# Chunk-causal encoder block: the queries of the next pair of heads are projected, split and stacked before the attention of the current pair

## Chip, cores and metric

One core of one Trainium2 chip runs the whole kernel in one launch. The metric is the device time of that launch in microseconds (us). Three runs of the kernel before have a median of 711.69 us (704.27 to 712.39).

## The reference, cut to what matters

One layer of an encoder on 512 tokens of width 1024. A modulated norm gives `u`; `u @ w_in` gives the inputs of a retention branch and of a sparse-attention branch ("DSA"); both go through output projections and gates into `w_o`; then comes a mixture of 16 experts and a last norm. The change touches the sparse attention alone. For a block of 128 queries it computes:

```python
kg = jax.vmap(lambda a, i: a[i])(k, sel)      # the selected keys
logits = jnp.einsum('bqhd,bqkd->bqhk', qb, kg).astype(jnp.float32) * (dh ** -0.5)
logits = logits + jnp.transpose(bias, (0, 1, 3, 2))
logits = jnp.where(valid[:, :, None, :], logits, -jnp.inf)
p = jax.nn.softmax(logits, axis=-1).astype(vg.dtype)
return jnp.einsum('bqhk,bqkd->bqhd', p, vg)
```

There are 8 heads of 64 columns, one latent key and value set for all heads, and 512 queries and keys. The queries of the heads are `u @ w_in[:, C_DQ:]`.

## The kernel before, in words

Everything is recorded first and ordered afterwards. Code in `block` calls engine operations through `Engine`; `Program.record` notes each one with its dependences and with a priority, which is its place in the recording plus `R.shift`. `Program.run` then plans: it takes each engine's ready operations by time and priority, with a cost for each instruction and each transfer written in the kernel, gives buffers their places, and issues all instructions from one line (L494). So every instruction has the line L494 in the profile, every SBUF tile is called `arena`, every PSUM tile `banks`, and a group is told by its shape. An engine works through its instructions strictly in the planned order. Nearly all transfers are issued by SyncE (SP), in one planned order as well.

Weights come from memory in float32, 1 MB at a time (`chunk`). `split` turns a chunk into two float16 halves (high and low): per 1024 columns one ScalarE (ACT) copy and one VectorE (DVE) subtraction. A product is then three float16 matmuls (`mm3`), and a projection of 128 columns for all 512 tokens is 24 matmuls of 128x512 (`z_T`).

The stage around the change (lines 961 to 1064) runs over four pairs of heads, and `dsa(pr, wqh, wql)` does one pair:

- `z_T` projects the pair's queries into a PSUM bank (line 964: 24 matmuls), and `hi_lo_psum` (line 966) writes the high half with ACT and the low half with DVE.
- `stack_q` (line 967) moves both halves into the stacked tile `dq` by four SBUF-to-SBUF transfers of 64 KB, so that one matmul with 128 rows multiplies the high and the low half together. In the profile these are `arena<-arena` transfers.
- A 0.5 MB transfer loads the pair's bias (line 969).
- For each of four blocks of 128 queries: four logit matmuls into a single double bank (lines 977, 978; tile `tL`, one buffer), bias added on DVE (980), mask and maximum on DVE (984), two exponentials (987) and two scalings (991) on ACT, transposes on TensorE (996), copies on ACT (997), and products with the values on TensorE (1000). The shapes of a block are 128x128, 128x256, 128x384 and 128x512 wide, since later queries see more keys.

Between these the planner lays other work, recorded after `dsa(pr)` with a later priority: `ret_out(pr)` (two new weight chunks, `w_gate` and `w_ret_out`; per pair 48 matmuls of the gates and 48 of the retention output, with a tanh) and two `mod_row` (each loads 2 MB of `w_ada` and sums it on DVE). After the four pairs come the second half of the gates with `w_dsa_out`, then `w_o`, the router and the experts. There are two buffers each for `dq`, for the halves (`tDH`) and for the PSUM banks of `psa`, which are given out in the order of recording. The loop before:

```python
    for pr in range(4):
        if pr % 2 == 0:
            wq = chunk([w_in[:, :, C_DQ + pr * 128:C_DQ + (pr + 2) * 128]])
        dsa(pr, *wq)
        R.shift, R.patience = 300, 0.0
        ret_out(pr)
        R.shift = 250
        for q in range(2):
            mod_row(pr, q)
        R.shift, R.patience = 0, 25
```

Of the kernel before, what the change touches and what calls it, by code (L numbers as in the profile page):

```python
# [31 lines left out]
C_RQ, C_RK, C_RV, C_RG, C_DQ, C_DKV, C_IQ, C_IK, C_IW, C_END = (  # L32
    0, 512, 1024, 2048, 3072, 3584, 3712, 4224, 4288, 4296)
# [470 lines left out]
def block(ctx, tc, A, out):  # L504
# [13 lines left out]
    def stt(o, a, s, b, op0, op1, **k):  # L518
        return DVE.scalar_tensor_tensor(o, a, s, b, op0=op0, op1=op1, **k)
# [18 lines left out]
    w_in = A["w_in"].rearrange("l (k p) n -> p (l k) n", p=128)  # L538
# [78 lines left out]
    def psa():  # L617
        return T(tA, [512])

    def psf():  # L620
        return T(tF, [512])
# [22 lines left out]
    def raw_tile():  # L644
        return T(tW8, [2048], F32, "raw", 1)

    def split(raw, n=2048, tag=tW8):
        hl = T(tag, [2, 2048], F16, "hl")
        wh, wl = hl[:, 0], hl[:, 1]
        for a in range(0, n, 1024):  # L650
            b = min(n, a + 1024)
            r, h, l = raw[:, a:b], wh[:, a:b], wl[:, a:b]
            ACT.activation(h, r, AF.Copy, scale=WS)
            stt(l, r, WS, h, OP.mult, OP.subtract)
        return wh, wl

    def chunk(parts, tag=tW8):
        raw = raw_tile()
        n = 0
        for src in parts:  # L660
            m = src.shape[1] * src.shape[2]
            SP.dma_start(raw[:, n:n + m].rearrange("p (k n) -> p k n", n=src.shape[2]), src)
            n += m
        return split(raw, n, tag=tag)
# [19 lines left out]
    for c in "aaawwawwwwww":  # L684
        if c == "a":
            ra = T(tADA, [8, 2, 256])
            n = len(ada) * 256
# [44 lines left out]
    for j in range(KT):  # L732
        wh, wl = split(wr[j], 712)
        for m in range(6):
            a, n = m * 128, widths[m]
# [24 lines left out]
    def hi_lo_psum(ps, scale, hi, lo):  # L760
        ACT.activation(hi, ps, AF.Copy, scale=scale)
        stt(lo, ps, scale, hi, OP.mult, OP.subtract)

    def stack_q(dst, hi, lo):
        SP.dma_start(dst[0:64, 0], hi[0:64])
        SP.dma_start(dst[64:128, 0], lo[0:64])
        SP.dma_start(dst[64:128, 1], lo[64:128])
        SP.dma_start(dst[0:64, 1], hi[64:128])
# [7 lines left out]
    def z_T(wh, wl, c0, cn, ps):  # L776
        for k in range(KT):
            mm3(ps, wh[:, k * cn + c0:k * cn + c0 + 128], wl[:, k * cn + c0:k * cn + c0 + 128],
                uh[:, k], ul[:, k], k == 0, k == KT - 1)
# [178 lines left out]

    R.patience = 25

    def dsa(pr, wqh, wql):
        dq = T(tDQ, [2, S], F16)
        p = psa()
        z_T(wqh, wql, (pr % 2) * 128, 256, p)
        hl = T(tDH, [2, S], F16)
        hi_lo_psum(p, IWS, hl[:, 0], hl[:, 1])
        stack_q(dq, hl[:, 0], hl[:, 1])
        bt = T(tBT, [2, S])
        SP.dma_start(bt, bass.AP(tensor=bias_rep.tensor, offset=bias_rep.offset + 2 * pr * 640 + 127,
                                 ap=[[8 * 640 - 1, 128], [640, 2], [1, S]]))  # L970
        po = psa()
        for b in range(NT):
            W = 128 * (b + 1)
            p = T(tL, [2, 512])
            for i in range(2):
                q = dq[:, i, b * 128:(b + 1) * 128]
                PE.matmul(p[:, i, :W], q, dkh[:, :W], start=True, stop=False)
                PE.matmul(p[:, i, :W], q, dkl[:, :W], start=False, stop=True)
            t = T(tLG, [2, S])
            stt(t[:, :, :W], p[:, :, :W], 0.125, bt[:, :, 384 - 128 * b:512], OP.mult, OP.add)  # L980
            sm = T(tSX, [3, 2])

            for i in range(2):
                DVE.tensor_tensor_reduce(t[:, i, :W], t[:, i, :W], am[b], scale=-1.0, scalar=BIG, op0=OP.add, op1=OP.min,
                                         accum_out=sm[:, 0, i:i + 1])
            for i in range(2):
                ACT.activation(t[:, i, :W], t[:, i, :W], AF.Exp, bias=sm[:, 0, i:i + 1], scale=-1.0,
                               accum_out=sm[:, 1, i:i + 1])
            DVE.reciprocal(sm[:, 2], sm[:, 1])
            for i in range(2):  # L990
                ACT.activation(t[:, i, :W], t[:, i, :W], AF.Copy, scale=sm[:, 2, i:i + 1])
            pT = T(tPT, [2, S])
            for i in range(2):
                pt = T(tPTP, [512])
                for k in range(b + 1):
                    PE.transpose(pt[:, k * 128:(k + 1) * 128], t[:, i, k * 128:(k + 1) * 128], ident)
                ACT.activation(pT[:, i, :W], pt[:, :W], AF.Copy)
            for k in range(b + 1):
                for i in range(2):
                    PE.matmul(po[64 * i:64 * i + 64, b * 128:(b + 1) * 128], dvf[:, k], pT[:, i, k * 128:(k + 1) * 128],  # L1000
                              start=k == 0, stop=k == b)
        hi_lo_psum(po, 1.0, oth[:, pr], otl[:, pr])
# [14 lines left out]
    def ret_out(m2):  # L1017
        gw = chunk([wg[:, :, m2 * 256:(m2 + 1) * 256]])
        rw = chunk([wro[:, :, m2 * 256:(m2 + 1) * 256]])
        for m in (2 * m2, 2 * m2 + 1):  # L1020
            g = gates(gw, m, 56, 1)
            p = psf()
            for k in range(KT):
                s = slice(k * 256 + (m % 2) * 128, k * 256 + (m % 2) * 128 + 128)
                mm3(p, rw[0][:, s], rw[1][:, s], rth[:, k], rtl[:, k], k == 0, k == KT - 1)
            stt(yt[m // 4][:, m % 4], g, 1.0, p, OP.add, OP.mult)
# [6 lines left out]
    def mod_row(v, q):  # L1033

        c0 = (2 + v) * D + q * 512
        acc = T(tMA, [2, 512])
        SP.dma_start(acc[0:1, 1], A["b_ada"][:, c0:c0 + 512])
        for u in range(2):
            ra = T(tMR, [4, 512])
            SP.dma_start(ra, w_ada[:, u * 4:u * 4 + 4, c0:c0 + 512])  # L1040
            for t in range(4):
                w = silw[:, u * 4 + t:u * 4 + t + 1]
                if u + t == 0:
                    DVE.tensor_scalar(acc[:, 0], ra[:, t], w, None, op0=OP.mult)
                else:
                    stt(acc[:, 0], ra[:, t], w, acc[:, 0], OP.mult, OP.add)
        hl = T(tMH, [2, 512], F16)
        ACT.activation(hl[:, 0], acc[:, 0], AF.Copy)
        DVE.tensor_sub(hl[:, 1], acc[:, 0], hl[:, 0])
        p = T(tF, [512], F32, "mod")  # L1050
        for i in range(2):
            PE.matmul(p, ones16, hl[:, i], start=i == 0, stop=i == 1)
        stt(acc[0:1, 1], p[0:1], IWS, acc[0:1, 1], OP.mult, OP.add)
        SP.dma_start(vec_row[v:v + 1, q * 512:(q + 1) * 512], acc[0:1, 1])

    for pr in range(4):
        if pr % 2 == 0:
            wq = chunk([w_in[:, :, C_DQ + pr * 128:C_DQ + (pr + 2) * 128]])
        dsa(pr, *wq)
        R.shift, R.patience = 300, 0.0  # L1060
        ret_out(pr)
        R.shift = 250
# [3 lines that stand above are left out]
# [19 lines left out]
    def psm():  # L1085
        return T(tB4, [512])
# [81 lines left out]
    for t in range(NT):  # L1168
# [69 lines left out]
        pr = psm()  # L1238
# [161 lines left out]
    with tc.If(nr > 1):  # L1400
        for t in range(NT):
            SP.dma_start(mrow[t * 128:(t + 1) * 128, :], h3s[t][:, 0])
        with tc.For_i(1, nr):
            DVE.tensor_scalar(rank, rank, -float(SL), None, op0=OP.add)
            pr, pg = psf(), psf()
# [61 lines left out]
```

## Time and profile before

| what | value |
|---|---|
| median of three runs (lowest to highest) | 711.69 us (704.27 to 712.39) |
| the profiled execution | 714.36 us |
| its span, first to last instruction | 712.3 us |
| TensorE (PE) busy in the span | 635.0 us (89%) |
| VectorE (DVE) busy | 515.4 us (72%) |
| ScalarE (ACT) busy | 337.5 us (47%) |
| mean granted TensorE clock | 0.957 of full speed |

The profile gives for every instruction its start and length in microseconds from the start of the span, and the idle time before it in square brackets with what ended it. PE is the matmul part of TensorE. A float16 matmul's own length overlaps with its neighbours, so a stretch's busy time divided by its count is what one costs. A granted clock of 1.00 is 2.4 GHz and 0.50 is 1.2 GHz.

### The profile page before, as it was taken

Reading aid. Unit: us, or ns where it says so; the run is one execution under the profiler, and the core shown is the slowest. Engines: PE = TensorE matmul, PEld = TensorE weight load, DVE = VectorE, ACT = ScalarE, POOL = GpSimd, SP = SyncE. Lnnn points to the kernel's source line nnn. Section 1 sums busy time; section 2 is a strip of 40 time slices with the busy share of each in tenths; the row PEclk is TensorE's granted clock in tenths of the full one; section 3 lists DMA queues with packets and bytes.
Section 4 is the critical chain, followed back from the end, with each engine's and each line's share of the span. In section 5 each row is a group of like instructions: output and inputs, shape, how many; then the busy total and the mean of one; then the engine's idle time right before and its main releaser. Section 6 shows DMA issues by size and latency. Waiting matters only on the chain. (4 is left out here: it accounts for less than half of the span.)

```text
span 712.3 us, 12336 instructions
## 1 busy us (share of the span) xinstructions
PE 635.0 (89%) x4793; PEld 372.0 (52%) x4793; DVE 515.4 (72%) x1026; ACT 337.5 (47%) x564; POOL 86.8 (12%) x79
## 2 busy tenths in 40 slices
PE   3799998989999899999799899997858897999874
PEld 2345465747566545454354344444456475776631
DVE  3998699999995668898588545578883644775536
ACT  5448622434243346864385333334445543665414
POOL 1001010111011100000000000021123330115403
PEclk9799999999999999999999999999969899999986
DMA  9998625263265378747758532943437999999753
GB/s 301 359 331 250 178 64 155 64 209 101 48 208 167 84 252 246 244 145 269 227 178 305 201 125 86 337 174 124 155 121 234 326 348 340 369 347 363 190 175 118
DMA packets 84048, 151.67 MB, mean 213 GB/s; under 512 B 9316, under 2 KB 49717, under 8 KB 83858
## 3 DMA queue, kind: packets, MB, share of 16 engines
q1 hardware_dynamic: 80690, 143.21, 60.6%
q0 software_dynamic: 3248, 7.63, 4.6%
q8 instruction: 39, 0.64, 0.4%
q14 instruction: 23, 0.19, 0.1%
q10 hardware_dynamic: 48, 0.00, 0.0%
HBM read 135.42 MB, written 14.45 MB: 210 GB/s over the span
## 5 line engine op out<-in xcount | busy, mean ns | idle before, releaser
L494 PE MATMUL banks<-arena 128*128 128x512 f16 (+9 forms) x4793 | 635.0, 295 | 67.8 <-DVE arena L494 37.1
L494 PEld LDWEIGHTS <-arena 128*128 128x128 f16 (+1 forms) x4118 | 294.7, 100 | 237.2 <-issue 43.5
L494 ACT ACTIVATE arena<-arena 128x1024 f16<-128x1024 f32 (+10 forms) x295 | 231.3, 824 | 228.2 <-DVE arena L494 111.4
L494 DVE SCALAR_TENSOR_TENSOR arena<-arena 128x1024 f16<-128x1024 f32 (+7 forms) x288 | 258.2, 919 | 63.6 <-ACT arena L494 50.3
L494 DVE SCALAR_TENSOR_TENSOR arena<-banks,arena 96x512 f32<-96x512 f32 (+11 forms) x151 | 89.1, 608 | 76.6 <-PE banks L494 52.7
L494 ACT ACTIVATE arena<-banks 128x512 f32<-128x512 f32 (+9 forms) x162 | 84.3, 575 | 99.9 <-PE banks L494 98.9
L494 PEld LDWEIGHTS banks<-arena 128*128 128x128 f32 (+3 forms) x675 | 82.6, 168 | 93.0 <-DVE arena L494 36.8
L494 POOL TENSOR_TENSOR arena<-arena 128x512 f32<-128x512 f32 (+2 forms) x36 | 40.9, 1137 | 305.9 <-DVE arena L494 251.4
L494 DVE TENSOR_TENSOR arena<-arena 128x512 f16<-128x512 f32 (+7 forms) x104 | 58.7, 575 | 8.5 <-ACT arena L494 4.1
L494 ACT ACTIVATE arena<-banks,arena 128x128 f32<-128x128 f32 (+1 forms) x48 | 22.9, 531 | 40.2 <-DVE arena L494 24.2
L494 POOL DMA_INDIRECT hrow<-arena x14 | 26.3, 1882 | 39.1 <-DVE arena L494 22.0
L494 DVE TENSOR_SCALAR arena<-arena 128x1 f32<-128x1 f32 (+8 forms) x81 | 22.5, 290 | 11.3 <-ACT arena L494 5.5
L494 DVE MAX8 arena<-arena 128x8 f32<-128x256 f32 (+3 forms) x52 | 27.5, 530 | 1.4
L494 POOL DMA_INDIRECT arena<-u2row,arena x15 | 18.0, 1198 | 79.3 <-PE banks L494 64.2
L494 DVE MATCH_REPLACE8 arena<-arena 128x256 f32<-128x256 f32 (+3 forms) x56 | 27.2, 487 | 0.0
L494 DVE SCALAR_TENSOR_TENSOR arena<-arena,banks 128x512 f32<-128x512 f32 x17 | 11.6, 686 | 18.6 <-PE banks L494 16.9
L494 POOL IOTA arena<- 128x4 int32 (+2 forms) x3 | 0.9, 297 | 196.8 <-PE banks L494 191.4
L494 DVE CUSTOM_DVE_ANT_0 arena<-arena 128x128 f32<-128x128 f32 (+3 forms) x32 | 14.3, 482 | 0.0
L494 ACT ACTIVATION_READ_ACCUMULATOR arena<-arena 128x1 f32 x56 | 10.5, 188 | 0.0
L494 DVE TENSOR_TENSOR arena<-arena,banks 128x512 f32<-128x512 f32 (+1 forms) x12 | 6.1, 513 | 5.4 <-PE banks L494 5.4
L494 DVE BATCH_NORM_STATS2 arena<-banks 128x6 f32<-128x128 f32 x32 | 7.1, 283 | 2.7 <-PE banks L494 2.6
L494 DVE MATCH_VALUE_LOAD arena<-arena 128x8 f32 x56 | 5.0, 88 | 1.2
(19 smaller groups left out, 26.3 us busy)
## 6 DMA issues: line engine op xcount, KB each, us to landing
arena<-in_w_ada SPq DMA_DIRECT2D x16, 1024.0 KB
arena<-in_w_exp_gate SPq DMA_DIRECT2D x32, 512.0 KB
arena<-in_w_exp_up SPq DMA_DIRECT2D x32, 512.0 KB
arena<-in_w_exp_down SPq DMA_DIRECT2D x16, 1024.0 KB
arena<-in_w_in SPq DMA_DIRECT2D x14, 1024.0 KB
arena<-in_w_ada SPq DMA_DIRECT2D x4, 2048.0 KB
arena<-in_w_gate SPq DMA_DIRECT2D x8, 1024.0 KB
arena<-arena SPq DMA_DIRECT2D x112, 64.0 KB
```

The lines of the kernel that those rows point to most:

```text
L494: o.call(*[self.real(x) for x in o.args], **{n: self.real(x) for n, x in o.kw.items()})
```

## The change

`dsa` is cut in two: `dsa_q` (projection, split, stacking) and `dsa` (bias and attention). The loop records `dsa_q` one pair ahead: those of pairs 0 and 1 before the attention of pair 0, then that of pair 2 before the attention of pair 1 and that of pair 3 before the attention of pair 2. The second query chunk is so recorded before `ret_out(1)` too. No operation is added or removed, and no size changes.

```diff
-    def dsa(pr, wqh, wql):
+    def dsa_q(pr, wqh, wql):
         dq = T(tDQ, [2, S], F16)
         p = psa()
         z_T(wqh, wql, (pr % 2) * 128, 256, p)
         hl = T(tDH, [2, S], F16)
         hi_lo_psum(p, IWS, hl[:, 0], hl[:, 1])
         stack_q(dq, hl[:, 0], hl[:, 1])
+        return dq
+
+    def dsa(pr, dq):
         bt = T(tBT, [2, S])
...
+    dqs = []
     for pr in range(4):
-        if pr % 2 == 0:
-            wq = chunk([w_in[:, :, C_DQ + pr * 128:C_DQ + (pr + 2) * 128]])
-        dsa(pr, *wq)
+        while len(dqs) < min(pr + 2, 4):
+            n = len(dqs)
+            if n % 2 == 0:
+                wq = chunk([w_in[:, :, C_DQ + n * 128:C_DQ + (n + 2) * 128]])
+            dqs.append(dsa_q(n, *wq))
+        dsa(pr, dqs[pr])
         R.shift, R.patience = 300, 0.0
         ret_out(pr)
```

The planner orders the whole stage anew; the orders of SP and ACT show what moves. First SP's queue at the start of the stage, before. `64x512` are the stackings, `in_w_ada` and `in_w_gate` weights of 1 MB, `bias_rep` the bias; the four stackings are those of pair 0.

```order
L494 DMA arena<-in_w_ada 128x4x512
L494 DMA arena<-bias_rep 128x2x512
L494 DMA arena<-in_b_ada 1x512
L494 DMA arena<-arena 64x512 x2
L494 DMA arena<-in_w_ada 128x4x512
L494 DMA arena<-arena 64x512 x2
L494 DMA arena<-bias_rep 128x2x512
```

The same place after the change; the eight stackings are those of pairs 0 and 1, one of pair 1 standing between the two halves of pair 0.

```order
L494 DMA arena<-in_w_ada 128x4x512
L494 DMA arena<-in_w_gate 128x8x256
L494 DMA arena<-bias_rep 128x2x512
L494 DMA arena<-in_b_ada 1x512
L494 DMA arena<-arena 64x512 x8
L494 DMA arena<-bias_rep 128x2x512
L494 DMA arena<-in_w_ada 128x4x512 x2
```

The 1 MB that stood between the halves of pair 0 now follows them, and the gate weights of `ret_out(2)` stand ahead of them. Next, SP's queue at the stackings of pair 3 (the last four `64x512` of the stage), before:

```order
L494 DMA arena<-in_w_gate 128x8x256
L494 DMA arena<-in_w_ada 128x4x512
L494 DMA arena<-in_w_dsa_out 128x4x512
L494 DMA arena<-arena 64x512 x4
L494 DMA arena<-in_w_ada 128x4x512
```

And after:

```order
L494 DMA arena<-in_w_gate 128x8x256
L494 DMA arena<-in_w_ada 128x4x512
L494 DMA arena<-in_b_ada 1x512
L494 DMA arena<-in_w_ret_out 128x8x256
L494 DMA arena<-arena 64x512 x4
L494 DMA arena<-in_w_ada 128x4x512 x2
L494 DMA vec_row<-arena 1x512
L494 DMA arena<-in_w_gate 128x8x256
```

They now stand ahead of pair 2's attention, behind the weights of `ret_out(3)`; the logit matmuls of pair 3 come about 150 TensorE instructions later. Last, ACT's order at the start of pair 2's attention, before. `128x1024` is a weight split of `ret_out(3)`'s gate chunk, `128x128 x2` are the exponentials and then the scalings of the first block:

```order
L494 ACTIVATE arena<-banks 128x512 x3
L494 ACTIVATE arena<-banks,arena 128x512
L494 ACTIVATE arena<-arena 128x128 x2
L494 ACTIVATE arena<-arena 128x1024
L494 ACTIVATE arena<-arena 128x128 x2
L494 ACTIVATE arena<-arena 128x256
```

And after, where `banks 128x512` is the high half of pair 3's queries and the two `128x1024` behind it are that gate chunk:

```order
L494 ACTIVATE arena<-arena 128x1024
L494 ACTIVATE arena<-banks 128x512
L494 ACTIVATE arena<-arena 128x1024 x2
L494 ACTIVATE arena<-arena 128x128 x2
L494 ACTIVATE arena<-arena 128x256
L494 ACTIVATE arena<-arena 128x128 x2
```

Both splits of the gate chunk now stand ahead of the pair's first exponentials.

## Rows read from the trace of the kernel before

**Rows 1.** The page: busy us of each engine (share of the span) and instructions.

```profile
PE 635.0 (89%) x4793; PEld 372.0 (52%) x4793; DVE 515.4 (72%) x1026; ACT 337.5 (47%) x564; POOL 86.8 (12%) x79
```

**Rows 2.** Windows: stretch, length; PE, PEld, DVE, ACT, POOL busy; clock, DMA share, GB/s.

```profile
250.00:375.00 125.00, 117.27 (x671) 60.10 (x670) 98.74 (x194) 76.07 (x170) 0.71 (x1) 0.99 0.69 225
375.00:460.00 85.00, 83.06 (x386) 37.54 (x384) 48.75 (x61) 31.55 (x40) 0.21 (x1) 1.00 0.59 203
532.00:655.00 123.00, 111.54 (x1565) 80.12 (x1562) 68.97 (x79) 62.08 (x80) 30.67 (x22) 0.94 0.97 329
```

**Rows 3.** Waits of PE, 230 to 400: total us, times, longest.

```profile
PE banks L494 <- DMA arena<-arena: 9.1, 5, 4.4
...
PE banks L494 <- ACT arena L494: 0.2, 1, 0.2
```

**Rows 4.** Timeline of PE at the first logits of pairs 0, 1, 3: start, us.

```profile
250.79 8.80 PE L494 MATMUL banks<-arena 128*128 128x512 f16 x42
261.02 0.46 PE L494 MATMUL banks<-arena 128*128 128x128 f16 x4 [1.44 <-DMA arena<-arena]
...
285.68 0.82 PE L494 MATMUL banks<-arena 128*128 128x128 f16 x5 [1.63 <-DMA arena<-arena]
...
331.72 13.98 PE L494 MATMUL banks<-arena 128*128 128x512 f16 x64
350.10 5.09 PE L494 MATMUL banks<-arena 128*128 128x128 f16 x20 [4.41 <-DMA arena<-arena]
```

**Rows 5.** Windows around the wait of pair 3 (columns as in rows 2).

```profile
336.00:349.00 13.00, 9.69 (x45) 4.20 (x43) 7.56 (x10) 3.81 (x5) 0.00 (x0) 1.00 0.99 313
350.80:354.20 3.40, 3.40 (x11) 1.37 (x10) 2.85 (x7) 1.38 (x5) 0.00 (x0) 0.50 0.06 24
```

**Rows 6.** Timeline of SP's issues, pair 0 and then pair 3.

```profile
254.47 0.54 SPq L494 DMA_DIRECT2D arena<-in_w_ada  x1
255.10 1.13 SPq L494 DMA_DIRECT2D arena<-arena  x2
...
304.03 0.59 SPq L494 DMA_DIRECT2D arena<-in_w_gate  x1
...
332.99 0.37 SPq L494 DMA_DIRECT2D arena<-in_w_gate  x1
337.06 0.37 SPq L494 DMA_DIRECT2D arena<-in_w_ada  x1
337.52 0.45 SPq L494 DMA_DIRECT2D arena<-in_w_dsa_out  x1
338.80 2.99 SPq L494 DMA_DIRECT2D arena<-arena  x4
```

**Rows 7.** Timeline of ACT: weight splits that waited, and one pair's first block.

```profile
287.65 0.40 ACT L494 ACTIVATE arena<-arena 128x128 f32<-128x128 f32 x1 [0.85 <-DVE arena L494]
289.14 1.09 ACT L494 ACTIVATE arena<-arena 128x128 f32<-128x128 f32 x3 [0.60 <-DVE arena L494]
310.10 2.04 ACT L494 ACTIVATE arena<-arena 128x1024 f16<-128x1024 f32 x4 [0.67 <-DMA arena<-in_w_gate]
340.49 2.52 ACT L494 ACTIVATE arena<-arena 128x1024 f16<-128x1024 f32 x3 [1.72 <-DMA arena<-in_w_gate]
349.45 2.00 ACT L494 ACTIVATE arena<-arena 128x1024 f16<-128x1024 f32 x2 [5.41 <-DMA arena<-in_w_dsa_out]
```

**Rows 8.** PE by shape, 250 to 360: busy us, mean ns.

```profile
L494 PE MATMUL banks<-arena 128*128 128x384 f16 x16 | 3.3, 326 | 0.0
L494 PE MATMUL banks<-arena 128*128 128x256 f16 x16 | 2.7, 295 | 0.0
L494 PE MATMUL banks<-arena 128*128 128x128 f16 x16 | 2.1, 220 | 7.5 <-DMA arena<-arena 7.5
```

**Rows 9.** Timeline of SP: the last issue before the experts' stream, and its first.

```profile
520.80 0.33 SPq L494 DMA_DIRECT2D u2row<-arena  x1
532.02 0.33 SPq L494 DMA_DIRECT2D arena<-in_w_exp_gate  x1
```

## Prediction

> **What bounds the kernel now.** I read the page first. TensorE is busy for 635.0 of the 712.3 us, more than any other engine [rows 1], so time is won only where it stands idle or runs slowly. The windows then show where the changed stage stands: between 250 and 375 us TensorE is busy for 117.27 of 125 us, DVE for 98.74, ACT for 76.07, and the transfer engines for 0.69 of the time [rows 2]. The reader is to see that this stage has 7.7 us of idle TensorE and no more, and that DVE and ACT have room. The stretch behind it, up to 460 us, has less than 2 us of idle TensorE.
>
> Who is waited for stands in the list of waits. Of PE's waits between 230 and 400 us, 9.1 us in five pieces end with an `arena<-arena` transfer, against 0.2 for ACT [rows 3]. By shape, 7.5 us of it stand before the logit matmuls of 128x128 [rows 8], which read the stacked queries; the other two pieces belong to the retention heads before the stage, which the change leaves alone. The timeline shows the three waits: 1.44 us at pair 0, 1.63 at pair 1, 4.41 at pair 3 [rows 4]. Pair 2 has none.
>
> Why pair 3's is the longest stands in SP's timeline. Its four stackings are issued from 338.80 to 341.79, behind three weight transfers of 1 MB from 332.99, 337.06 and 337.52 [rows 6]; the transfer engines are 0.99 busy from 336 to 349 us [rows 5]; and TensorE goes on at 350.10 [rows 4]. So 64 KB need some 8 us after the last issue, because they stand in a full queue. After that wait the clock drops: 3.4 us at a granted 0.50, that is 1.2 instead of 2.4 GHz, from 350.8 to 354.2 [rows 5]. The shorter waits of pairs 0 and 1 have no such stretch after them; the stage's mean clock is 0.99 [rows 2].
>
> **What the change removes.** No instruction or transfer is added or dropped, so only waits can move. For pairs 1, 2 and 3 the projection, the split into halves and the stacking now come one attention earlier. For pair 3 about 150 TensorE instructions stand between the projection and the logits, among them some 95 matmuls of 128x512. One of these costs 13.98 / 64 = 0.218 us [rows 4], so at least 20 us pass, where the slowest stacking of before needed 11.3 us, from its first issue at 338.80 to 350.10 [rows 4, 6]. The stack wait goes at pairs 1 and 3: 1.63 + 4.41 us. The slow clock behind pair 3's wait goes with it: 3.4 us at half speed did 1.7 us of work, so 1.7 us. Pair 0 has nothing ahead of it to hide behind but pair 1's projection; its 1.44 us are counted as removed here and its new wait below. Removed: 1.44 + 1.63 + 4.41 + 1.7 = 9.2 us.
>
> **What is late next.** Four places.
>
> *Pair 0.* Before, 54 projection and output matmuls stand between the retention heads' last products and the first logits, now 51, so TensorE arrives 3 x 0.218 = 0.65 us earlier: its run that ended at 250.79 + 8.80 = 259.59 [rows 4] would end at 258.9. Before, the last halves were issued from 255.10, behind 2.5 MB in SP's order (`w_ada`, bias, and `w_ada` again at 254.47), and were there at 261.02 [rows 4, 6]. Now 2.5 MB stand ahead too, but the late 1 MB is replaced by the gate chunk, which stands ahead of the bias, and a part of pair 1 stands between. The wait is at most 261.0 - 258.9 = 2.1 us, when nothing comes sooner, and 0 when the earlier start of the bulk is passed on. I take 1.0, the middle: no row decides it.
>
> The Trainium skill (DMA: Bandwidth & Descriptors, "Queues, rings and completion order") says that descriptors are consumed in ring order on each engine. By it alone pair 0's halves wait for the same 2.5 MB and this wait is kept; the sum by it has 2.1 us here and 5.5 in all. The rows agree that 64 KB wait behind the bulk (8 us at pair 3); that the bulk is now issued sooner is why less is taken.
>
> *Pair 2.* ACT now has both splits of `ret_out(3)`'s gate chunk ahead of the pair's first exponentials. What is queued behind that wait on ACT are the exponentials, the scalings, and through them the transposes on TensorE. From the chunk's issue to those transposes TensorE has 24 + 17 matmuls of 128x512, 41 x 0.218 = 9.0 us, and the logits of three blocks, (2.1 + 2.7 + 3.3) / 4 = 2.0 us [rows 8]: 11.0 us. After the chunk's landing ACT needs 2.0 us for two splits (the row of 349.45) and 2.6 us from the first exponential to the last of the three instructions behind it (287.65 to 289.14 + 1.09) [rows 7]: 4.6 us. So TensorE waits for L - 6.4 us, where L is the time from issue to landing. The same chunk had L = 310.10 - 304.03 = 6.1 [rows 6, 7]: no wait. Other chunks of 1 MB had 7.5 (332.99 to 340.49) and 11.9 (337.52 to 349.45), so it can reach 5.5. I take 0.
>
> *Pair 3, first block.* Here the first chunk of the second gates stands ahead of the exponentials in the same way, with again 41 matmuls and three blocks of logits to cover it: L - 6.4. The same chunk had L = 7.5: 1.1 us (0 to 5.5).
>
> *Pair 3, later blocks.* The `w_dsa_out` chunk is split between the third block's exponentials and scalings. It had L = 11.9 behind a full queue; now fewer transfers stand ahead, since the stackings and two gate chunks have moved forward, and the outputs of `ret_out(3)` lie over it. Between 0 (an L of 7.5 is covered) and 4.1 (L as before) I take 0.5.
>
> Could a new place gain? The work is the same, so no; only the 1.9 us of idle TensorE behind the stage could go as well [rows 2], as a gain of at most 1.9. I count none.
>
> Sum: 9.2 - (1.0 + 0 + 1.1 + 0.5) = 6.6 us less. Against the profiled execution, 714.36, that is 707.8 us. The median shown is 711.69, 2.7 us below that execution, so a median run comes to 711.69 - 6.6 = 705.1 us. Behind the stage every engine keeps its order but for some swaps up to 460 us, and the shift is passed on: the experts' stream starts at 532.02 after SP stood since 520.80 [rows 9], waiting for buffers that computing frees, so it starts earlier with the computing.
>
> The Trainium skill (DMA: Bandwidth & Descriptors, "Latency and other measured facts") puts the fixed cost of a transfer at about 2 us. By that, pair 3's stackings would have landed by 344, before TensorE ran out of work at 345.7, and there would be nothing to remove: the sum would be 0 at that pair. The rows differ by 6 us and decide: the queue in front, not the fixed cost, is what the change hides.
>
> **The rivals.**
>
> *Half of it.* Pairs 0 and 1 keep what they lose: pair 0 waits the full 2.1 us and ACT's early splits cost pair 1 as much as its 1.63. Then 4.41 + 1.7 - 0.7 - 1.6 = 3.8 us less, 707.9 us. For it: a chunk of this stage can take 11.9 us to land. Against it: pair 1's queries are stacked an attention ahead, and one such took 24.7 us before (261.02 to 285.68) [rows 4]. Chance 0.15.
>
> *The gain is lost in the experts' stage.* From 532 to 655 us the transfer engines are 0.97 busy at 329 GB/s [rows 2]; if that stream is not moved, an earlier attention stage ends in a longer wait there: 711.7 us. Against it: SP's gap of 11.2 us before it [rows 9], which ends with a freed buffer. Chance 0.12.
>
> *Slower.* ACT is the place, and L the price. If the two chunks at the beginnings of pairs 2 and 3 land as late as `w_dsa_out` did, 11.9 us, TensorE waits 5.5 us at each. Such waits are longer than the 4.41 us behind which the clock fell, so 1.7 us come with each. New: 1.0 + 2 x (5.5 + 1.7) + 0.5 = 15.9 us against 9.2 removed: 6.7 us slower, 718.4. It decides from 1.5 + 2 x (L - 6.4) = 9.2, L = 10.3 us. For it: one of the three landings read is above that. Against it: that one stood behind a queue in which several transfers of the stage's end met; the same two chunks had 6.1 and 7.5. Chance 0.13.
>
> That the change doesn't do what it says is no rival of its own: the orders show the stackings moved.
>
> **How the numbers follow.** The forecast, 705.1 us, has 0.60. Its own range goes from nothing new plus the 1.9 us behind (711.7 - 11.1 = 700.6) to an L of 8 at both chunks (4.7 us new, 707.2). The runs before scatter by 7.4 us below and 0.7 above their median, so the low end is set to 698, which leaves out little. The high end is 714: the lost gain and a small part of the slower case are inside. Within 2% of 711.69 is 697.5 to 725.9, about what a measurement of this kernel can tell from no change. Faster than that needs more than is there to be removed, but for a low run: 0.04. Slower than that needs twice the slower rival's price: 0.03. Same: 0.93.
>
> **What would show it right or wrong.** In the profile after, PE's waits should have no `arena<-arena` piece of over 0.5 us after pair 0's first logits, and none at pair 3. The stretch at half clock near 350 us should be gone. Waits of PE for ACT, now 0.2 us in this stage, should come to 1 to 3 us, just behind a split that waited for `in_w_gate`. The start of the experts' stream should lie 5 to 8 us earlier than 532. The prediction is wrong if PE's waits for ACT grow to over 6 us, if a new stretch at half clock shows in the stage, or if the stage is shorter and the end is not.

## The result, and the profile after

The changed kernel took 703.93 us (median of 20 runs, 698.02 to 712.03) beside 709.98 us of the kernel before (median of 20, 701.17 to 715.97): a ratio of 0.9935, 95% interval [0.9911, 0.9959]. The forecast was 6.6 us less; the medians differ by 6.05 us, and the ratio makes it 4.6. Ratios, here and below, leave out executions over 1.5% above the fastest of their kernel (most of all in the comparison with the delayed kernel: ten of 17 of the kernel before, none of the delayed one), while medians leave out none, so the two can differ.

The page after, busy us (compare [rows 1]):

```profile
PE 634.2 (90%) x4793; PEld 372.8 (53%) x4793; DVE 516.1 (73%) x1026; ACT 338.2 (48%) x564; POOL 87.6 (12%) x79
```

The work is the same. The windows after, moved with the stage (columns as in [rows 2]; the last row is a piece of the stretch that stood around 350 us in [rows 5]):

```profile
250.00:368.00 118.00, 116.91 (x681) 60.73 (x680) 99.20 (x202) 78.32 (x172) 1.01 (x1) 1.00 0.75 246
368.00:453.00 85.00, 84.20 (x391) 37.95 (x390) 51.43 (x63) 31.61 (x39) 0.21 (x1) 1.00 0.57 201
350.00:354.00 4.00, 4.00 (x26) 2.07 (x25) 3.77 (x6) 3.36 (x6) 0.00 (x0) 1.00 1.04 358
```

In the first stretch 7.73 us of idle TensorE have become 1.09, and from 350 to 354 us it runs at 1.00 where it had 0.50. The waits of PE after, 230 to 400 us:

```profile
PE banks L494 <- DMA arena<-arena: 2.9, 3, 1.8
PE banks L494 <- ACT arena L494: 0.8, 1, 0.8
PE banks L494 <- DVE arena L494: 0.5, 1, 0.5
```

Of the five `arena<-arena` waits of [rows 3] three are left. Two belong to the retention heads ahead of the stage (1.80 and 0.59 us, below), one to pair 0. The one wait for ACT lies behind the stage, at 396. The timeline of PE after, at pair 0 and at pair 3 (compare [rows 4]):

```profile
261.11 1.26 PE L494 MATMUL banks<-arena 128*128 128x128 f16 x8 [0.55 <-DMA arena<-arena]
...
327.68 9.67 PE L494 MATMUL banks<-arena 128*128 128x512 f16 x47
337.89 7.30 PE L494 MATMUL banks<-arena 128*128 128x256 f16 x38 [0.55 <-DVE arena L494]
```

Pair 0 waits for 0.55 us. Pair 3's first logits are inside the run of 47 matmuls and wait for nothing; 0.55 us for DVE before its second block is all that came new. Three issues of SP after, the stackings of pairs 0 and 1, those of pair 3 and the first gate chunk behind the attention (compare [rows 6]), and ACT's wait for that chunk (compare [rows 7]):

```profile
254.89 6.30 SPq L494 DMA_DIRECT2D arena<-arena  x8
...
305.52 2.38 SPq L494 DMA_DIRECT2D arena<-arena  x4
...
328.71 0.37 SPq L494 DMA_DIRECT2D arena<-in_w_gate  x1
```

```profile
334.59 2.52 ACT L494 ACTIVATE arena<-arena 128x1024 f16<-128x1024 f32 x3 [4.08 <-DMA arena<-in_w_gate]
```

Pair 3's stackings are the four issues from 305.52, some 30 us ahead of its logits instead of 11. ACT does stand 4.08 us before the gate chunk's split, as was feared, and TensorE has work meanwhile.

**The stage and what lies around it, in three profiles each.** To compare executions, the trace was cut by the number of the matmul on TensorE, of which both kernels have 4793: the stage is from the end of the 1301st to that of the 2101st, and the experts begin at the 2801st. The three windows of before (the given profile and two more, called `before_again` and `before_third` below), each a fence:

```profile
243.31:393.49 150.18, 142.45 (x802) 73.27 (x800) 119.77 (x230) 86.67 (x184) 1.01 (x1) 0.99 0.69 226
```

```profile
243.34:392.85 149.51, 142.21 (x801) 73.21 (x800) 119.78 (x230) 86.70 (x184) 1.01 (x1) 0.99 0.69 226
```

```profile
243.65:392.70 149.05, 142.84 (x801) 73.60 (x800) 119.76 (x230) 86.66 (x184) 1.01 (x1) 0.98 0.69 227
```

And after (the profile above, `after_again` and `after_third`):

```profile
244.93:385.77 140.84, 139.75 (x802) 72.77 (x800) 117.48 (x228) 85.00 (x182) 1.01 (x1) 1.00 0.71 236
```

```profile
247.87:389.38 141.51, 139.74 (x801) 72.79 (x800) 118.00 (x228) 85.14 (x183) 1.01 (x1) 1.00 0.71 235
```

```profile
244.47:385.19 140.72, 139.74 (x802) 72.73 (x800) 117.77 (x228) 84.98 (x182) 1.01 (x1) 1.00 0.71 236
```

The first number is where the stage begins, the third its length, the fourth TensorE's busy time in it. The stage takes 149.6 us on average before and 141.0 after: 8.6 us less, in every profile. But it begins at 243.4 before and at 245.8 after: 2.3 us are lost ahead of it. At the start of the experts (the 2801st matmul ends at 528.1, 524.1 and 524.9 before, at 519.0, 520.6 and 518.7 after) 6.2 us are left, and the medians of the timed runs differ by 6.05. The ends of the same six executions differ by less: the spans are 712.3, 706.6 and 705.2 us before and 706.6, 705.6 and 703.2 after, 2.9 us on average.

**What was lost ahead of the stage.** SP's issues before, from 209 to 234 us:

```profile
209.73 0.53 SPq L494 DMA_DIRECT2D arena<-in_w_gate  x1
212.31 14.02 SPq L494 DMA_DIRECT2D arena<-arena  x12
226.43 0.53 SPq L494 DMA_DIRECT2D arena<-in_w_ret_out  x1
227.06 5.71 SPq L494 DMA_DIRECT2D arena<-arena  x8
232.87 0.53 SPq L494 DMA_DIRECT2D arena<-in_w_in  x1
```

and after:

```profile
210.38 0.53 SPq L494 DMA_DIRECT2D arena<-in_w_in  x1
212.95 13.80 SPq L494 DMA_DIRECT2D arena<-arena  x12
226.85 0.53 SPq L494 DMA_DIRECT2D arena<-in_w_gate  x1
227.48 6.47 SPq L494 DMA_DIRECT2D arena<-arena  x8
234.05 0.53 SPq L494 DMA_DIRECT2D arena<-in_w_ret_out  x1
```

The `in_w_in` here is the second chunk of query weights, that of pairs 2 and 3 (the last load of `in_w_in` in both kernels). It has moved from behind the retention heads' last stackings to ahead of the last twenty of these transfers, and the gate chunk now stands between them in place of `in_w_ret_out`. All these loads are 1 MB, so it is not the amount ahead of the stackings that grew. The eight are issued over 6.47 us instead of 5.71, since the last of them waits, by the profile, until the load ahead of the eight has landed. SP's waits from 226 to 235 us, before and then after (total us, times, longest):

```profile
SPq L494 <- DMA arena<-in_w_ret_out: 0.8, 1, 0.8
```

```profile
SPq L494 <- DMA arena<-in_w_gate: 1.6, 1, 1.6
```

From the issue of that load to the issue of the last stacking it took 5.7 to 6.3 us with `in_w_ret_out` (seven profiles, those of the experiments below included) and 6.5 to 7.4 with `in_w_gate` (six). Why the gate chunk lands later is not shown.

What TensorE makes of it, in its timeline and in the window from 235 to 240 us (columns as in [rows 2]), before:

```profile
232.85 0.38 PE L494 MATMUL banks<-arena 128*128 128x512 f16 x1 [1.16 <-DMA arena<-arena]
233.73 1.46 PE L494 MATMUL banks<-arena 128*128 128x512 f16 x9 [0.50 <-DMA arena<-arena]
236.48 4.89 PE L494 MATMUL banks<-arena 128*128 128x128 f32 x31 [1.29 <-DVE arena L494]
```

```profile
235.00:240.00 5.00, 3.71 (x27) 2.92 (x27) 3.38 (x12) 1.70 (x2) 0.00 (x0) 1.00 0.53 182
```

and after:

```profile
234.13 0.38 PE L494 MATMUL banks<-arena 128*128 128x512 f16 x1 [1.80 <-DMA arena<-arena]
235.10 6.16 PE L494 MATMUL banks<-arena 128*128 128x512 f16 x32 [0.59 <-DMA arena<-arena]
```

```profile
235.00:240.00 5.00, 4.90 (x25) 3.44 (x26) 3.60 (x6) 1.56 (x3) 0.00 (x0) 0.66 0.64 210
```

The wait is 1.80 instead of 1.16 us, and the window behind it has a mean clock of 0.66 instead of 1.00: 0.34 x 5 = 1.7 us lost. In this profile the later wait for DVE is gone under the slower matmuls. All three profiles of after have this half clock and none of before; in `after_again` it goes on to 243 us and costs 3.4 us.

### The profile page after: what moved, and what is told of

Same layout as the page of the kernel before. It is cut to its first block, busy times and chain, and to the rows that moved or that the text cites. A ratio compares the mean times of both kernels' runs of the same rounds, so it can differ in the third digit from the quotient of the medians.

```text
span 706.6 us, 12348 instructions
## 1 busy us (share of the span) xinstructions
PE 634.2 (90%) x4793; PEld 372.8 (53%) x4793; DVE 516.1 (73%) x1026; ACT 338.2 (48%) x564; POOL 87.6 (12%) x79
## 5 line engine op out<-in xcount | busy, mean ns | idle before, releaser
L494 DVE SCALAR_TENSOR_TENSOR arena<-banks,arena 96x512 f32<-96x512 f32 (+10 forms) x151 | 88.9, 609 | 76.8 <-PE banks L494 53.4
```

Source lines behind the costliest of these rows:

```text
L494: o.call(*[self.real(x) for x in o.args], **{n: self.real(x) for n, x in o.kw.items()})
```

## The experiments

Run beside the changed kernel and the kernel before were two halves of the change, the stackings on another queue, and a delay put back.

**The change again.** No edit.

> The changed kernel once more, for a second profile. Theory: the attention stage has no wait for the stacked queries of pairs 1 to 3 again and no half clock, so its TensorE idle time is 1 to 2 us (before 7.7). Of the 10 us that the first profile saved up to 460 us, 2.7 were lost at the start of the experts, where TensorE waited 5.7 us for gathered rows (before 1.7) and the clock was low for longer. If that is chance, this profile has a wait of 1 to 3 us there and the span is about 8 to 9 us under 712; if it belongs to the change, 5 to 6 us again and a span near 706. Ratio of times 0.990 to 0.996 either way.

Measured: 703.4 us (median of 12) against 709.27 (29 runs), ratio 0.9922 [0.9886, 0.9958], the first result once more. The stage is 141.51 us, the wait at pair 0 is 1.24 us. TensorE waited 5.4 us for gathered rows at the start of the experts, as in the first profile.

> The kernel before once more, for a second profile. Theory: the same three waits for the stacked queries within 0.5 us (1.4, 1.6, 4.4 us) and the half clock behind the third. If the wait for gathered rows at the start of the experts (1.7 us in the first profile) is chance, it can be anything from 1 to 6 us here; if the change lengthens it, it is below 2.5 us.

Measured: one execution of 708.62 us. The three waits are 1.16, 2.43 and 3.71 us, the last two outside the 0.5 us that were given; the half clock behind pair 3 costs 1.7 again. The wait for gathered rows is 5.5 us here; with 4.2 and 2.4 in the third profiles of before and after it is scatter and not the change.

**Only pair 3 ahead.**

```diff
-        while len(dqs) < min(pr + 2, 4):
+        while len(dqs) < (1, 2, 4, 4)[pr]:
```

> Only the queries of pair 3 are made one attention ahead; pairs 0, 1 and 2 as before. Theory (the wait of pair 3 and the half clock behind it carry the gain): 4.4 + 1.7 us less, the waits of pairs 0 and 1 stay at 1.4 and 1.6 us: ratio 0.990 to 0.994. Rival (the gain comes from the new order of the stage as a whole, not from this wait): less than a third of the gain, ratio 0.997 to 1.001.

Measured: 705.83 us (12 runs) against 709.27, ratio 0.9979 [0.9937, 1.0022]; by medians 3.4 us less. The stage:

```profile
243.30:386.60 143.30, 140.34 (x802) 73.18 (x800) 118.91 (x229) 84.69 (x183) 1.01 (x1) 1.00 0.70 235
```

It is 6.3 us shorter, as the waits were (pair 0 kept 1.34, pair 1 0.56, pair 3 none; one new wait for ACT of 1.05 us), and it begins where it did before. The stage did what the theory said. The timed ratio did not: it lies in the rival's range, the interval reaches down to 0.9937, and the median's 0.995 is between the two.

**Only pair 1 ahead.**

```diff
-        while len(dqs) < min(pr + 2, 4):
+        while len(dqs) < (2, 2, 3, 4)[pr]:
```

> Only the queries of pair 1 are made ahead of the attention of pair 0; pairs 2 and 3 as before. Theory: the wait of pair 1 goes (1.6 us), the wait of pair 3 of about 4.4 us and the half clock behind it stay: ratio 0.996 to 1.000. Rival (new order as a whole): the full gain, ratio 0.991 to 0.994, with a short wait at pair 3 too.

Measured: 705.14 us (12 runs), ratio 0.9948 [0.992, 0.9975]: more than the theory gave it, less than the rival, and the interval reaches into both. It also overlaps that of the whole change, so the runs do not show that the whole is faster than this half. The stage:

```profile
243.80:387.05 143.25, 139.78 (x802) 72.94 (x800) 120.45 (x230) 88.25 (x185) 1.01 (x1) 1.00 0.70 232
```

Pair 1's wait is gone and pair 0's is 1.69; but pair 3's, which this kernel does not touch, is 1.78 instead of 4.41, with no half clock behind it. Its SP timeline shows what stands ahead of the stackings now, and its PE timeline the wait:

```profile
330.75 0.37 SPq L494 DMA_DIRECT2D arena<-in_w_gate  x1
...
331.70 0.37 SPq L494 DMA_DIRECT2D arena<-in_w_ada  x1
332.16 0.46 SPq L494 DMA_DIRECT2D arena<-in_w_dsa_out  x1
336.03 0.37 SPq L494 DMA_DIRECT2D arena<-in_w_ada  x1
338.20 2.48 SPq L494 DMA_DIRECT2D arena<-arena  x4
```

```profile
346.96 2.22 PE L494 MATMUL banks<-arena 128*128 128x128 f16 x14 [1.78 <-DMA arena<-arena]
```

The stackings go out at 338.20, as before (338.80). Ahead of them, three of the four transfers of 1 MB were issued 6 us or more earlier and only one in the last 3 us, where before there were two within 1.8 us [rows 6]. They need 8.8 us from first issue to logits instead of 11.3. This points to how much bulk is still on its way when the small transfers are issued, and the parts of the change do not add up: 6.3 and 6.3 us make 8.6 together.

**The stackings on another queue.** In the kernel before, `stack_q` gets a queue as an argument, and the call for the selected-key queries gives GpSimd's (in a second kernel, ACT's):

```diff
-    def stack_q(dst, hi, lo):
-        SP.dma_start(dst[0:64, 0], hi[0:64])
-        SP.dma_start(dst[64:128, 0], lo[0:64])
-        SP.dma_start(dst[64:128, 1], lo[64:128])
-        SP.dma_start(dst[0:64, 1], hi[64:128])
+    def stack_q(dst, hi, lo, q=None):
+        q = q or SP
+        q.dma_start(dst[0:64, 0], hi[0:64])
+        q.dma_start(dst[64:128, 0], lo[0:64])
+        q.dma_start(dst[64:128, 1], lo[64:128])
+        q.dma_start(dst[0:64, 1], hi[64:128])
...
-        stack_q(dq, hl[:, 0], hl[:, 1])
+        stack_q(dq, hl[:, 0], hl[:, 1], POOL)
```

> The kernel before, with the sixteen stackings of the selected-key queries issued from GpSimd's queue instead of SP's; nothing else is moved. Theory (the 64 KB wait behind the 1 MB weight transfers that stand ahead of them in SP's queue): the waits ahead of the logits at pairs 0, 1 and 3 (1.44, 1.63 and 4.41 us before, 7.5 in all) fall to under 2 us in all, the stretch at half clock near 350 us is gone (1.7 us), and the time falls by 5 to 7 us, a ratio of 0.990 to 0.993, as the change does. Rival (it is the 16 transfer engines that are full, whichever queue a transfer is issued from): over 5 us of the waits stay, and the ratio is 0.998 to 1.002.

Measured: 705.99 us (12 runs) against 708.62 (35 runs), ratio 0.9977 [0.9942, 1.0011]. The waits fell to 1.11 + 0 + 1.01 = 2.1 us and the half clock at pair 3 is gone. The windows of the stage and of pair 3's stackings, then GpSimd's issue and PE's wait there in the timelines:

```profile
244.81:388.94 144.13, 141.24 (x802) 73.22 (x800) 119.90 (x230) 87.04 (x184) 9.70 (x17) 1.00 0.71 235
338.70:347.30 8.60, 7.59 (x37) 3.33 (x36) 4.79 (x6) 2.96 (x4) 2.05 (x4) 1.00 1.01 321
```

```profile
338.70 2.05 POOL L494 DMA_DIRECT2D arena<-arena  x4 [27.82 <-ACT arena L494]
```

```profile
346.78 0.27 PE L494 MATMUL banks<-arena 128*128 128x128 f16 x2 [0.80 <-DMA arena<-arena]
347.26 2.03 PE L494 MATMUL banks<-arena 128*128 128x128 f16 x12 [0.21 <-DMA arena<-arena]
```

Issued at the same time as before (338.70), the stackings are there by 347.26 instead of 350.10: 3 us sooner. The other 8.6 us stay in a queue of its own, while the transfer engines are busy for 1.01 of the time, as the rival has it. For this queue the trace also tells the time from issue to landing. The last number is the median us of the four stackings, at pair 2 and then at pair 3:

```profile
arena<-arena POOLq DMA_DIRECT2D x4, 64.0 KB, 2.1
```

```profile
arena<-arena POOLq DMA_DIRECT2D x4, 64.0 KB, 6.8
```

At pair 2 the transfer engines are 0.80 busy from the first issue to the last landing, and one load of 1 MB was issued in the 3 us ahead; at pair 3 they are 1.01 busy, with two loads in the last 1.7 us. The same 64 KB took 2.1 or 6.8 us by what else the engines had to move. Theory and rival each hold a part. The stage is 5.5 us shorter, 1.4 of which is lost ahead of it (a half clock like the change's, in this profile); the end shows 2.6 by medians, less than the theory's 5 to 7.

> As the run before it, with the sixteen stackings issued from ACT's queue. Theory: as there, waits of under 2 us in all, less what ACT loses by sixteen issues (at some 0.6 us each 10 us of ACT, which has 40 us of idle time in this stage), so a ratio of 0.990 to 0.996. Rival (full transfer engines): over 5 us of the waits stay, ratio 0.998 to 1.004.

Measured: 708.07 us (10 runs), ratio 1.0032 [0.9994, 1.007]. The waits are 1.00, 0, 2.32 (at pair 2, which had none) and 2.02 us, 5.3 in all, with no half clock; the stage is 147.38 us. Waits and ratio are the rival's. The order of the stage is another one here as well, since the planner costs ACT's issues, so the run does not tell the queue's part from that of the order.

**The change, and the stackings on GpSimd's queue as well.** The same edit in the changed kernel; a second kernel also gives the retention heads' queries and keys to that queue.

> The changed kernel, with the stackings of the selected-key queries issued from GpSimd's queue. Only pair 0's wait (0.55 and 1.24 us in two profiles) is left to win in the stage: theory: it falls to under 0.5 us, and the ratio to the kernel before is 0.990 to 0.993, 0 to 1 us better than the change alone. Rival (full transfer engines): pair 0's wait stays at 0.5 to 1.3 us and the ratio is that of the change, 0.992 to 0.994.

Measured: 709.04 us (12 runs) against 708.62, ratio 1.0042 [0.9999, 1.0085]. Both missed. The stage:

```profile
243.88:387.21 143.33, 140.65 (x802) 72.81 (x800) 116.82 (x227) 85.37 (x182) 9.51 (x17) 1.00 0.70 229
```

Pair 0 still waits for 0.51 and 0.27 us. The stage is 2.3 us longer than the change's: 1.4 of it is idle time, most of it new waits for DVE (1.52 at pair 0's second block), and 0.9 longer busy time.

> The changed kernel with the stackings of the selected-key queries and those of the retention heads' queries and keys issued from GpSimd's queue. The profile of the kernel after has 2.4 us of waits for stacked tiles ahead of the stage (1.80 and 0.59) and 3.4 us at half clock behind them (1.7 us lost). Theory: these go too, 3 to 4 us beside the change's 5: ratio 0.986 to 0.990. Rival (full transfer engines, or GpSimd's queue blocked by what stands in it ahead): the waits stay or grow, and the ratio is 0.992 to 1.000.

Measured: 709.34 us (12 runs), ratio 1.0034 [0.9994, 1.0074], above both ranges. The waits for the retention heads' stackings are gone, and so is the half clock behind them: the stage begins at 241.10, 4.7 us sooner than after the change. But it takes 144.40 us, with 3.3 us of waits for DVE. At the start of the experts this kernel is the earliest of all (518.54), and yet its time is that of the kernel before.

> The changed kernel with the stackings on GpSimd's queue once more, to see where it loses what its stage won. If the loss is in the experts' stage: the stage takes 143 to 144 us as in its first profile and the stretch from the first expert's weights to the end is longer than the 180 us of that profile by 4 us or more. Rival (the first profile's stage was lucky): the stage itself takes over 146 us, with waits for stackings or for DVE.

Measured: one execution of 709.62 us. The stage is 144.16 us, and from SP's first expert weights (527.18) to the end of the span (707.7) it takes 180.5 us, beside 702.8 - 524.91 = 177.9 in the first profile: longer, but by 2.6 us and not by 4. The stage, near the first case's 143 to 144, explains 2.3 to 3.1 us of the 5.1 by which this kernel's median lies above the change's 703.93; the rest was not found.

**A delay put back.** One matmul of the first product behind the gates is issued 40 times more in front of itself (`EXTRA_AT` is 2213, counted in recorded operations).

```diff
+        npe = 0
         for o in order:
             o.done = True
+            npe += o.eng == "PE"
+            if o.eng == "PE" and npe == EXTRA_AT:
+                for _ in range(40):
+                    o.call(*[self.real(x) for x in o.args], **dict({n: self.real(x) for n, x in o.kw.items()}, stop=True))
             o.call(*[self.real(x) for x in o.args], **{n: self.real(x) for n, x in o.kw.items()})
```

> The changed kernel with 40 extra matmuls of 128x512 on TensorE just behind the gates and the output projection that follow the attention (one matmul is repeated in front of itself, so that its result is as it was): 40 x 0.218 = 8.7 us put back at the end of the stage that the change shortened by 8 to 9 us. Theory (what is won in the stage is passed on to the end in full): 8.7 us more than the changed kernel, so 703.7 + 8.7 = 712.4 us and a ratio to the kernel before of 1.002 to 1.007. Rival (the experts' stage gives some of a gain back, or takes some of a delay in, since its weights stream at the transfer engines' pace): only 5 to 6 us more, the time of the kernel before, ratio 0.997 to 1.001.

Measured: 711.63 us (12 runs), 7.7 us over the 703.93 of the first result (some 5 to 10 by the scatter of the runs); ratio to before 1.0086 [1.0034, 1.0137], medians 711.63 to 710.56 (17 runs). The window with the 40 matmuls:

```profile
410.77:462.57 51.80, 51.80 (x241) 23.48 (x240) 26.78 (x33) 17.46 (x23) 0.21 (x1) 1.00 0.62 223
```

It is 8.63 us longer than the same stretch of after without them (43.17). The ratio lies above both ranges, and its interval reaches into the theory's only; the medians make it 1.0015, between the two ranges. So most of a delay at that place comes through to the end; the rival's 5 to 6 us are not excluded.

**The third profiles.**

> The kernel before once more, for a third profile. The waits ahead of the logits and the half clock behind pair 3 come as in the two others (7.3 to 7.5 us and 3.4 us at 0.50): the stage from the first of its matmuls to the last takes 149 to 151 us. Rival (they are an accident of one execution): under 147 us.

> The changed kernel once more, for a third profile: the same stage takes 140 to 142 us, with one wait for a stacking of 0.5 to 1.3 us, at pair 0. Rival (the gain is an accident): over 144 us.

Measured: 149.05 us and 140.72 us, with 6.2 us of waits for stackings before (4.16 at pair 3) and 0.42 after, at pair 0, both under what was given. The half clock behind pair 3 costs 3.4 us in that profile of before, twice what it did in the two others.

## Why the prediction was right

The sum was 6.6 us, the measurement 6.05 by medians. The mechanism was right inside the stage. But two of its steps were off, the new waits behind ACT and the stretch ahead of the stage, and that their errors cancelled was luck.

- **Removed, 9.2 us: right.** Waits of 7.5, 7.3 and 6.2 us and half clocks of 1.7, 1.7 and 3.4 us stand in the three profiles of before: 9.3 us on average. After, no half clock is left in the stage, and of the waits only pair 0's.
- **Pair 0, 1.0 us: right in size.** 0.55, 1.24 and 0.42 us in the three profiles and 1.57 in the delayed kernel, all within the 0 to 2.1 given. The 1.0 was the middle of that range, and no row decided it. The rule of the Trainium skill that was weighed there (DMA: Bandwidth & Descriptors, "Queues, rings and completion order"), ring order alone, gave 2.1; the rows after show less.
- **Pairs 2 and 3 behind ACT, 0 + 1.1 + 0.5 us: over-sized.** Nothing contradicts the rule L - 6.4, but L was less. Pair 3's gate chunk was issued at 328.71 and split at 334.59: L = 5.9, under the 6.4 that TensorE can cover, and no wait came; ACT's 4.08 us cost nothing. The 1 to 3 us of waits for ACT that were named as a sign did not come. L = 7.5 had been taken from a chunk that stood in the old crowd of transfers. A term which depends on a landing time has to be sized with the queue of the new order, not of the old. In place of the 1.6 came some 0.55 us for DVE, in each of the three profiles.
- **"The work is the same": slightly under.** Of the 8.6 us by which the stage became shorter 5.8 are idle time (7.1 to 1.3 on average), 2.3 slow clock, and 0.5 shorter busy time of the same matmuls, which is not told apart further.
- **The retention heads' waits "which the change leaves alone": wrong.** This step failed: it read the new order inside the stage only. With pair 2's queries ahead, the second query chunk is recorded before `ret_out(1)`, and SP's queue changed from 210 us on, before the stage. The kernels with only pair 1 or only pair 3 ahead keep the old order there (`in_w_in` at 233.4 and 232.9) and begin the stage at 243.8 and 243.3; a kernel with pair 2 alone ahead was not run. In the new order the load that the last stacking waits for lands later, TensorE's first wait grew from 0.8 to 1.2 us to 1.6 to 2.1, and the clock fell behind it. Of the 2.3 us by which the stage begins later, 1.8 arise after the 1201st matmul (at some 222 us) and 0.6 ahead of it and of these waits. The half clock is in 5 of the 6 profiles of kernels that have SP's new order there (the three of after, the delayed one, and one of two with GpSimd's queue), and in 1 of the 7 that have the old one (three of before, the two halves, and the two kernels with stackings on another queue). By TensorE's first wait the same 13 profiles part cleanly: half clock behind all six of 1.59 to 2.53 us, behind none of the seven of 0.68 to 1.21.
- **Passed on: right at the start of the experts, not shown to the end.** The experts' first weights are issued at 532.0, 527.8 and 528.3 before, and at 522.6, 524.1 and 522.2 after: 6.4 us earlier on average (5 to 8 was said; the two first profiles alone show 9.4, because that of before ran late). Most of the delay that was put back came through. But the six profiled executions end only 2.9 us apart, and each half of the change has the experts begin as early as the whole (519.3 and 519.4), while its median fell by 3.4 and 4.1 us. So 6.2 us at the experts and 6.05 in the medians agree in part by chance.

Of the rivals, the slower one needed L = 10.3 and L was 5.9. Half of it would have kept pair 1's 1.63 us, which are gone. The gain wholly lost in the experts' stage is excluded for the change by its ratio's interval; that a part of it is lost there is not. The changed kernels on GpSimd's queue are 3.7 and 7.2 us earlier at the experts (522.0 and 518.5, against 525.7) and show no gain at the end in 12 runs each. Why stays open.

That it is the other transfers under way and not a fixed cost of each is shown by the 2.1 and 6.8 us from issue to landing in one execution, and by pair 3's stackings in three kernels: they took 11.3, 8.8 and 8.6 us from about the same time of issue (338.8, 338.2 and 338.7), the latter two with less bulk just in front or with a queue of their own. About 1 us of the difference is the issuing, which ends at 341.8, 340.7 and 340.8. The Trainium skill (DMA: Bandwidth & Descriptors, "Latency and other measured facts") has about 2 us as a transfer's fixed cost; the trace agrees at pair 2 on GpSimd's queue (2.1 us), but none of these three was there in that time, with the transfer engines busy for 0.92 to 1.01 of it.

## What to carry to other kernels

Small transfers that gate TensorE and share a queue with 1 MB weight loads are better issued a whole stage ahead; a queue of their own made them land only 3 us sooner here, of 11, since the transfer engines stay shared. When a load's consumer is recorded earlier, read where the load itself goes in the queue, and who stood there: here a load moved forward by 22 us, and the cost came some 10 us ahead of the stage that was changed. And where a wait is removed or grows, look at the granted clock behind it: in this kernel it added 1.7 to 3.4 us to the price.

## What was not expected of the hardware

**How short a pause went with a lower clock.** The prediction had the clock fall behind 4.41 us and not behind 1.4 or 1.6. Ahead of the stage after, it fell behind 1.80 and 0.59 us with one matmul between them (rows above), while 1.16, 0.50 and 1.29 us, as much in all, left it at 1.00. Length alone does not tell it either: 1.78 us at pair 3 of the kernel with only pair 1 ahead, and 2.43 at pair 1 of `before_again`, left it at 1.00.

**The end of the kernel has more than one length.** Its last 32 matmuls, the same in every kernel, in the first and in the third profile of before:

```profile
692.47 10.26 PE L494 MATMUL banks<-arena 96*128 96x512 f16 x32 [2.95 <-PEq L1400]
```

```profile
688.23 7.07 PE L494 MATMUL banks<-arena 96*128 96x512 f16 x32 [1.88 <-ACTq L1400]
```

They take 7.07 or 8.75 or some 10.2 us, behind a wait of 1.9 us or of 2.5 to 3.8. Their mean granted clock is 0.68 in the first profile, 0.80 in the second (8.75 us) and 1.00 in the third. That is 3 to 5 of the 10 us or more by which executions of one kernel differ, and both kernels have the short and the long ends. So one profile's time (708.52 us after) is no measure of the gain; the cut by matmul number is a better one for the stage.
